# Forty expert-key blocks in plain fp32 behind chosen one-hot groups, query weights read once for most tiles, paired compares

## The chip, the cores and the metric

The kernel runs on one core of a Trainium2 chip. The metric is device microseconds of one execution; every time below is in microseconds unless it says ns. PE is TensorE, DVE is VectorE, ACT is ScalarE, POOL is GpSimd, SP issues most of the plain DMAs.

## The reference, cut to what matters

The layer takes 512 latent tokens of width 1024, runs a state-space branch and a neighbourhood-attention branch, merges them, and then runs PEER, an expert retrieval with product keys. The change touches PEER alone:

```python
def peer_ffn(h, w_q, subkeys, u_tab, v_tab):
    q = (h @ w_q).reshape(b, l, PEER_HEADS, 2, PEER_HALF)          # 8 heads, 2 halves of 128
    s = jnp.einsum('blhnd,nkd->blhnk', q, subkeys)                 # 128 keys per half
    s_top, i_top = lax.top_k(s, PEER_TOPK)                         # 16 best of each half
    cand = s_top[..., 0, :, None] + s_top[..., 1, None, :]         # 256 sums
    cand_idx = i_top[..., 0, :, None] * PEER_KEYS + i_top[..., 1, None, :]
    best, pos = lax.top_k(cand, PEER_TOPK)
    expert = jnp.take_along_axis(cand_idx, pos, axis=-1)           # 16 of 16384 experts
    gate = jax.nn.softmax(best, axis=-1)
    a = einsum('td,thkd->thk', h_blk, u_tab[expert])               # per token, 128 experts
    w = gate * gelu(a)
    return einsum('thk,thkd->td', w, v_tab[expert])
```

## The kernel before, in words

The 512 tokens are four tiles of 128. Tiles 0 to 2 (`ND = 3`, `DT = 384` tokens) are computed densely: the kernel multiplies all 16384 rows of `u_tab` with the 384 tokens, 128 rows at a time, and masks. Tile 3 is done with gathers of single rows.

*Splitting.* A weight tile is loaded on SP's queue as plain fp32 into `wraw` (3 buffers) and split by `w_split` (L171) into two fp32r parts: ACT casts `hi` (L174), DVE subtracts to get `lo` (L175). `mm3` (L449) then does three fp32r matmuls per slice of 128 inputs (hi x hi, hi x lo, lo x hi), 24 for 8 slices. `w_ahead` and `w_next` (L180, L193) walk one fixed list `wseq`: they keep the loads two to three tiles ahead and the split one tile ahead.

*Order of the stage.* `h_part` (L937) transposes the normed tiles and writes `hth` and `htl`, the split of h. `scores(h, pair)` (L1003) projects a head's two query halves for a pair of tiles: it takes two weights of the list, so all 16 query weights are loaded and split twice, once per pair. It then multiplies with the sub-keys and DVE takes the 16 best with max, find-index and match-replace. `choose(t)` (L1034) does the second top-16 of a tile and turns positions into expert numbers; its compare (L1067) of 128 positions with 16 numbers writes 2048 bf16 elements, and a multiply (L1069) of the same size follows. The program runs `scores` of tiles 0 and 1, `choose(0)`, `choose(1)`, `scores` of tiles 2 and 3, then the one-hot groups.

*One-hot groups.* `g_group(q)` (L1117) makes the gate matrix of 8 tokens: four DVE operations on 128x1024 fp16 (L1129 to L1132) write three one-hot tiles `og` (two buffers each), 16 matmuls (L1141, L1142) make a 128x128 gate matrix per token, ACT writes them out (L1144) and a DMA on ACT's queue stores them in `Gt_d` (L1147). There are 3 x 16 = 48 groups. `choose(2)` and `choose(3)` are put behind groups 14 and 33.

*Blocks that run ahead.* `u_stage(j)` (L950) is one block: 128 rows of `u_tab` against the 384 tokens, gelu, into one slot of a ring of 41. Forty blocks (`LAG`) run ahead of the main loop: 8, 12 and 18 spread over the groups of tiles 0, 1 and 2 (`NU`) and not bound to any, and two bound behind the last group. The binding is `tc.issue_after(ins)`: the block's matmuls keep behind `ins` on its engine's queue. What isn't bound, the scheduler orders by its own simulated times.

*Main loop* (L1307). For j = 0 to 124 it reads a row block of `v_tab`, splits it, multiplies the ring slot with the gates (`gch`, read back from `Gt_d`), does 18 matmuls of 512 columns into six `acc` banks, runs `u_stage` of block j + 40, and issues some gathers on POOL for tile 3. The gathers' buffers lie where the one-hot tiles were.

The line that the blocks turn on:

```python
mm3(a[:, 0:DT], w, [t[:, 0:DT] for t in hth], [t[:, 0:DT] for t in htl], KD)
```

Of the kernel before, what the change touches and what calls it, by code (L numbers as in the profile page):

```python
# [48 lines left out]
LAG = 40  # L49

GLEAD = 32
G_IN_Q = lambda q: 0
UA = 0
WQE = lambda p, i: 0
# [22 lines left out]
UKEEP = 2  # L77
NTAIL = 3
CQ = (14,33)
CB = (1,1)  # L80
BT = 3
NU = (8,12,18)
# [4 lines left out]
def tile_hybrid(ctx, tc, A, out, dbg=None):  # L87
# [92 lines left out]
    def w_ahead(load_to, split_to, eng):  # L180
# [768 lines left out]

    def u_stage(j):  # L950
# [3 lines left out]
        mm3(a[:, 0:DT], w, [t[:, 0:DT] for t in hth], [t[:, 0:DT] for t in htl], KD)  # L954
# [48 lines left out]
    def scores(h, pair):  # L1003
        qs = []
        for n in range(2):
            w = w_next(("wq", 2 * h + n), gp if WQE(pair, 2 * h + n) else dve)
            a = bank()
            mm3(a[:, 0:256], w, [t[:, pair * 256:pair * 256 + 256] for t in hth],
                [t[:, pair * 256:pair * 256 + 256] for t in htl], KD)
            q_ = tk1.tile([128, 256], F32, tag="q_", name="q_", bufs=4)  # L1010
            act.copy(q_, a[:, 0:256])
            qs.append(q_)
        sp = bank("mc" if pair * 8 + h < SPN else "tp")
        for n, q_ in enumerate(qs):
            for t in range(2):
                pe.matmul(sp[:, n * 256 + t * 128:n * 256 + t * 128 + 128], q_[:, t * 128:(t + 1) * 128], subk[:, n],
                          start=True, stop=True)
        sca = tk1.tile([128, 2, 2, 128], F32, tag="sc", name="sc", bufs=2)
        act.copy(sca.rearrange("p n a b -> p (n a b)"), sp)
        for n in range(2):  # L1020
            sc = sca[:, n]
            if h == 0 and n == 0 and pair == 0:
                DBG("sc0", sc.rearrange("p a b -> p (a b)"))
            for z in range(2):
                t = pair * 2 + z
                s_, i_ = st[:, t, n, h], it[:, t, n, h]
                dve.max(s_[:, 0:8], sc[:, z])
                dve.max_index(i_[:, 0:8], s_[:, 0:8], sc[:, z])
                s2_ = tk1.tile([128, 128], F32, tag="s2_", name="s2_", bufs=2)
                dve.match_replace(s2_, s_[:, 0:8], sc[:, z], -3.0e38)  # L1030
                dve.max(s_[:, 8:16], s2_)
                dve.max_index(i_[:, 8:16], s_[:, 8:16], s2_)

    def choose(t):  # L1034
# [15 lines left out]
        pf, u_, ab = ti("pf"), ti("u_"), ti("ab", BF16, 2, NH, 16)  # L1050
# [6 lines left out]
        dve.tensor_scalar(ab[:, 0], u_, MAGIC, MAGIC, op0=ALU.add, op1=ALU.subtract)  # L1057
        dve.scalar_tensor_tensor(ab[:, 1], ab[:, 0], -16.0, pf, op0=ALU.mult, op1=ALU.add)
# [26 lines left out]
    for h in range(NH):  # L1085
        scores(h, 0)
# [101 lines left out]

    pend_u = 0

    def pend(n, bind=False):
        nonlocal pend_u
        for _ in range(n):
            if pend_u < LAG - UKEEP:
# [209 lines left out]
```

## Time and profile before

| what | value |
|---|---|
| median of 3 runs | 1843.59 us (1843.41 to 1844.24) |
| the profiled execution's own time | 1847.01 us |
| its span, first to last instruction | 1845.2 us |
| PE busy | 1724.4 us, 93% |
| PE weight loads busy | 1507.5 us, 82% |
| DVE busy | 1468.6 us, 80% |
| ACT busy | 782.4 us, 42% |
| POOL busy | 372.9 us, 20% |
| mean granted TensorE clock | 0.968 |
| bytes moved by DMA | 426.16 MB, mean 231 GB/s |

Shares of the whole span mix stages that have different limits. The view by stretches gives each engine's busy time in a part of the span, and the share of full speed that the chip granted to TensorE's clock there. In the groups by line a row is: line, engine, operation, written tile and read tiles, shapes, count, then busy time and mean duration, then the idle time of that engine just before those instructions and what ended it. In a timeline a row is start, duration, engine and line; rows that follow each other on an engine can be merged ("x4"). The ends of matmuls are modelled, so the distance between starts is the better price.

### The profile page before, as it was taken

The numbers are of one execution on the slowest core, as the hardware profiler recorded it, in microseconds if no ns is written. First come the engines' busy times: TensorE is split into PE (matmuls) and PEld (weight loads), VectorE is DVE, ScalarE is ACT, GpSimd is POOL, SyncE is SP. The second block draws the span as 40 slices with busy tenths as digits, with TensorE's granted clock in tenths as the row PEclk, the third lists the DMA queues.
The fourth block names the chain that finished last, engine by engine and source line by source line (L and its number), as shares of the span: only waits on it lengthen the run. The fifth ranks groups of instructions, "written<-read, shape, count | busy, mean of one in ns | idle before, by whom it ended". The sixth has DMA issues, their size and how long they took to land.

```text
span 1845.2 us, 27478 instructions
## 1 busy us (share of the span) xinstructions
PE 1724.4 (93%) x9941; PEld 1507.5 (82%) x9941; DVE 1468.6 (80%) x3041; ACT 782.4 (42%) x1220; POOL 372.9 (20%) x304
## 2 busy tenths in 40 slices
PE   5999899899999899995589999999999999999997
PEld 2878677777799799994579899999999999988885
DVE  8889765875689998999888788888878788794455
ACT  6452555432464346665423333333333333333333
POOL 0001000000000000000332344544445444440012
PEclk9999999999999999995699999999999999999998
DMA  8341362885634336765799799999999999994332
GB/s 332 95 134 59 97 170 49 282 285 164 210 130 149 115 121 187 209 196 166 228 392 348 266 344 354 323 340 342 331 337 350 341 328 344 327 337 138 127 114 80
DMA packets 186328, 426.16 MB, mean 231 GB/s; under 512 B 25552, under 2 KB 91216, under 8 KB 186192
## 3 DMA queue, kind: packets, MB, share of 16 engines
q1 hardware_dynamic: 84816, 231.44, 37.1%
q0 software_dynamic: 36864, 134.23, 20.2%
q10 hardware_dynamic: 64512, 58.73, 10.2%
q8 instruction: 78, 1.28, 0.3%
q14 instruction: 58, 0.48, 0.1%
HBM read 388.72 MB, written 35.62 MB: 230 GB/s over the span
## 4 chain that ended last, share of the span: by engine, by line
PE 64%; DVE 18%; DMA 9%; issue 5%; POOL 2%; ACT 2%; SPq 0%; ACTq 0%; DVEq 0%; POOLq 0%
PE acc L1276 8%; PE acc L1275 8%; PE acc L1277 8%; PE kk L447 4%; PE yy L445 4%; PE yy L447 4%; PE yy L446 4%; PE kk L446 4%; PE kk L445 4%; DVE wlo L175 3%; DMA wm<-in_wmodT_dram 3%; PE mm L445 2%; PE mm L447 2%; DMA gu<-in_pu_dram,idx 2%; PE mm L446 2%
## 5 line engine op out<-in xcount | busy, mean ns | idle before, releaser
L174 ACT CAST whi<-wraw 128x1024 fp32r<-128x1024 f32 (+1 forms) x212 | 213.8, 1009 | 222.6 <-PE mm L446 100.4
L1158 POOL DMA_INDIRECT gu<-in_pu_dram,idx x128 | 168.9, 1319 | 598.0 <-PE mm L1142 385.3
L175 DVE TENSOR_TENSOR wlo<-wraw,whi 128x1024 fp32r<-128x1024 f32 (+1 forms) x212 | 247.6, 1169 | 36.1 <-ACT whi L174 35.5
L1158 POOL DMA_INDIRECT gu<-in_pv_dram,idx x128 | 176.8, 1382 | 192.1 <-DVE gacc L1176 165.8
L1176 DVE SCALAR_TENSOR_TENSOR gacc<-gu,av,gacc 128x1024 f32<-128x1024 f32 x127 | 162.7, 1281 | 28.1 <-DMA gu<-in_pv_dram,idx 27.7
L1257 DVE TENSOR_TENSOR wlo<-wraw,whi 128x1024 fp32r<-128x1024 f32 x128 | 157.6, 1232 | 33.5 <-ACT whi L1256 33.0
L1165 DVE SCALAR_TENSOR_TENSOR gj<-gu,hrow 128x1024 bf16<-128x1024 f32 x128 | 156.2, 1220 | 33.9 <-DMA gu<-in_pu_dram,idx 33.8
L447 PE MATMUL kk<-hth,wlo 128*128 128x384 f32 x512 | 174.2, 340 | 3.4 <-DVE wlo L175 3.4
L445 PE MATMUL kk<-hth,whi 128*128 128x384 f32 x512 | 173.4, 339 | 2.4 <-ACT ring L956 2.4
L445 PE MATMUL yy<-hth,whi 128*128 128x384 f32 x512 | 173.0, 338 | 1.5 <-ACT whi L174 1.3
L446 PE MATMUL kk<-htl,whi 128*128 128x384 f32 x512 | 173.1, 338 | 0.0
L447 PE MATMUL yy<-hth,wlo 128*128 128x384 f32 x512 | 173.0, 338 | 0.0
L446 PE MATMUL yy<-htl,whi 128*128 128x384 f32 x512 | 172.4, 337 | 0.0
L1256 ACT CAST whi<-wraw 128x1024 fp32r<-128x1024 f32 x128 | 133.7, 1046 | 59.5 <-PE kk L446 26.7
L1144 ACT ACTIVATE gs<-mm 128x512 f32<-128x512 f32 x96 | 94.1, 1090 | 56.1 <-PE mm L1142 53.1
L447 PE MATMUL mm<-hxh,wlo 128*128 128x512 f32 x256 | 103.3, 404 | 11.4 <-DVE wlo L175 11.4
L445 PE MATMUL mm<-hxh,whi 128*128 128x512 f32 x256 | 101.6, 402 | 5.6 <-ACT whi L174 3.0
L446 PE MATMUL mm<-hxl,whi 128*128 128x512 f32 x256 | 102.5, 400 | 0.0
L447 PEld LDWEIGHTS kk<-hth,wlo 128*128 128x128 f32 x512 | 96.9, 189 | 5.4 <-DVE wlo L175 4.4
L445 PEld LDWEIGHTS kk<-hth,whi 128*128 128x128 f32 x512 | 97.0, 189 | 4.5 <-ACT ring L956 2.7
L445 PEld LDWEIGHTS yy<-hth,whi 128*128 128x128 f32 x512 | 96.4, 188 | 4.6 <-ACT whi L174 1.7
L446 PEld LDWEIGHTS kk<-htl,whi 128*128 128x128 f32 x512 | 97.0, 190 | 1.7
(1912 smaller groups left out, 4258.4 us busy)
## 6 DMA issues: line engine op xcount, KB each, us to landing
wraw<-in_puT_dram SPq DMA_DIRECT2D x128, 512.0 KB
wraw<-in_pv_dram SPq DMA_DIRECT2D x128, 512.0 KB
Gt_d<-gs ACTq DMA_DIRECT2D x24, 1024.0 KB
gch<-Gt_d ACTq DMA_DIRECT2D x32, 768.0 KB
wraw<-in_win_dram SPq DMA_DIRECT2D x32, 512.0 KB
wm<-in_wmodT_dram SPq DMA_DIRECT2D x32, 512.0 KB
wraw<-in_wq_dram SPq DMA_DIRECT2D x32, 512.0 KB
wm<-in_wm_dram SPq DMA_DIRECT2D x16, 512.0 KB
```

The source lines that it names most:

```text
L174: act.copy(hi[:, :kn], raw[:, :kn])
L175: i = eng.tensor_sub(lo[:, :kn], raw[:, :kn], hi[:, :kn].bitcast(F32))
L445: pe.matmul(o, hi[:, k], xh, start=(k == 0), stop=False)
L446: pe.matmul(o, hi[:, k], xl, start=False, stop=False)
L447: pe.matmul(o, lo[:, k], xh, start=False, stop=(k == kn - 1))
L1158: gp.indirect_dma_start(out=u, out_offset=None, in_=A[tab], in_offset=bass.IndirectOffsetOnAxis(ap=ix[:, s:s + 1], axis=0))
L1165: dve.scalar_tensor_tensor(jk, u, 1.0, hrow, op0=ALU.mult, op1=ALU.mult, accum_out=av[:, s:s + 1])
L1176: dve.scalar_tensor_tensor(gacc, u, av[:, s:s + 1], gacc, op0=ALU.mult, op1=ALU.add)
L1257: dve.tensor_sub(lo, w, hi.bitcast(F32))
L1275: pe.matmul(acc[t][half], wh_[:, ts], hi[:, cs], start=(j == 0), stop=False)
L1276: pe.matmul(acc[t][half], wh_[:, ts], lo[:, cs], start=False, stop=False)
L1277: return pe.matmul(acc[t][half], wl_[:, ts], hi[:, cs], start=False, stop=(j == 127))
```

## The change

- `u_stage`: for the first 40 blocks (`NF = 40`) the raw fp32 tile is used as it is, without a split, and one plain fp32 matmul per slice takes the place of the three. The plain h of the 384 tokens is kept in `h32`, in three buffers `hq` that were free by then; two of the eight slices lie in two pieces (256 and 128 columns). `h_part` writes it (for tile 2 by an extra ACT operation per slice).
- `scores(i, tiles)` does one weight for a list of tiles: the first 4 weights (`QSP`) for the pairs as before, the other 12 for all four tiles at once (matmuls of 512 columns).
- `choose`: `ab` holds each value twice, and the compare reads pairs, as the one-hot operations do.
- Order: all scores first, with three blocks behind weights 7, 10 and 13; then `choose(0)` and 4 blocks; then the groups. `choose(1)`, `(2)`, `(3)` are bound behind groups 8, 24 and 40, each with 4 blocks bound behind that group's last matmul; of the other groups every third has one block bound behind it. 4 blocks (`UKEEP`) are kept for after the last group.
- `gacc` is allocated at its first use, in the buffer of one of the `hq` tiles.

```diff
-    wseq += [("wq", i, KD) for i in range(2 * NH)]
-    wseq += [("puT", j, KD) for j in range(UA)]
-    wseq += [("wq", i, KD) for i in range(2 * NH)]
-    wseq += [("puT", j, KD) for j in range(UA, 128)]
+    wseq += [("wq", i, KD) for i in range(QSP)] * 2
+    for i in range(QSP, 2 * NH):
+        wseq.append(("wq", i, KD))
+        if i in US:
+            wseq.append(("puT", US.index(i), KD))
+    wseq += [("puT", j, KD) for j in range(len(US), 128)]
...
-            wsp[i] = w_split(wraw.pop(i), wseq[i][2], eng)
+            raw = wraw.pop(i)
+            wsp[i] = raw if wseq[i][0] == "puT" and wseq[i][1] < NF else w_split(raw, wseq[i][2], eng)
...
+    hq = [hxp.tile([128, D], F32, tag=f"hc{i + 1}", name=f"hq{i}") for i in range(3)]
+    h32 = [(hq[k // 2][:, k % 2 * DT:k % 2 * DT + DT],) for k in range(6)]
+    h32 += [(hq[2 * i][:, 768:], hq[1][:, 768 + 128 * i:896 + 128 * i]) for i in range(2)]
...
-            f = h23[:, k] if lo else x1p.tile([128, 256], F32, tag="hf2", name="hf2", bufs=2)
+            f = h23[:, k] if lo else h32[k][0][:, 0:256]
             act.activation(f, p[:, :n], AF.Identity, bias=mod[:, 24 + k:25 + k], scale=A2[:, k:k + 1])
+            if lo:
+                act.activation(h32[k][0][:, 256:384] if k < 6 else h32[k][1], p[:, :128], AF.Identity,
+                               bias=mod[:, 24 + k:25 + k], scale=A2[:, k:k + 1])
...
-        mm3(a[:, 0:DT], w, [t[:, 0:DT] for t in hth], [t[:, 0:DT] for t in htl], KD)
+        if j < NF:
+            for k in (0, 1, 2, 3, 4, 6, 7, 5):
+                c = 0
+                for f in h32[k]:
+                    n = f.shape[-1]
+                    pe.matmul(a[:, c:c + n], w[:, k], f, start=(k == 0), stop=(k == 5))
+                    c += n
+        else:
+            mm3(a[:, 0:DT], w, [t[:, 0:DT] for t in hth], [t[:, 0:DT] for t in htl], KD)
...
+    def scores(i, tiles):
+        h, n = divmod(i, 2)
+        c = slice(tiles[0] * 128, tiles[-1] * 128 + 128)
+        nt = len(tiles)
+        w = w_next(("wq", i), gp if WQE(i) else dve)
+        a = bank()
+        mm3(a[:, 0:nt * 128], w, [t[:, c] for t in hth], [t[:, c] for t in htl], KD)
...
-            dve.tensor_tensor(ov, ab[:, n].rearrange("p h (k o) -> p (h k) o", o=1).to_broadcast([128, 128, 16]),
-                              io16.rearrange("p (o e) -> p o e", o=1).to_broadcast([128, 128, 16]), op=ALU.is_equal)
+            dve.tensor_tensor(ov.rearrange("p x (e w) -> p x e w", w=2),
+                              ab[:, n].rearrange("p x (o w) -> p x o w", o=1).to_broadcast([128, 128, 8, 2]),
+                              io16.rearrange("p (o e w) -> p o e w", o=1, w=2).to_broadcast([128, 128, 8, 2]),
+                              op=ALU.is_equal)
...
-    for h in range(NH):
-        scores(h, 0)
+    for pair in ((0, 1), (2, 3)):
+        for i in range(QSP):
+            scores(i, pair)
...
-            if chq and q == CQ[chq[0] - 2]:
-                with tc.issue_after(omark[0]) if CB[chq[0] - 2] else ExitStack():
+            if chq and q == CQ[chq[0] - 1]:
+                with tc.issue_after(omark[0]):
                     choose(chq.pop(0))
-            pend((k + 1) * nu // n - k * nu // n, t >= BT)
-
-    choose(0)
-    choose(1)
-    pend(UA)
-    for h in range(NH):
-        scores(h, 1)
+                pend(CU, gmark[0])
+            elif q % GU == 0:
+                pend(1, gmark[0])
+
+    for i in range(QSP, 2 * NH):
+        scores(i, (0, 1, 2, 3))
+        pend(i in US)
     close_pool(t1cm)
     gpl_open()
+    choose(0)
+    pend(CU)
```

## Rows read from the trace of the kernel before

**Rows 1.** Stretches: busy us (instructions) by engine; granted clock, DMA share, GB/s.

```profile
500.00:630.00 130.00, 121.41 (x935) 116.87 (x935) 124.80 (x569) 65.39 (x108) 0.38 (x2) 0.98 0.42 135
630.00:820.00 190.00, 185.81 (x1329) 176.79 (x1329) 179.40 (x456) 113.20 (x146) 0.00 (x0) 1.00 0.57 168
820.00:910.00 90.00, 47.97 (x410) 41.00 (x409) 83.00 (x188) 48.58 (x55) 7.14 (x6) 0.61 0.61 181
910.00:941.00 31.00, 23.41 (x107) 21.83 (x106) 22.00 (x47) 9.03 (x12) 13.89 (x9) 0.83 1.02 386
941.00:1660.00 719.00, 716.37 (x3612) 650.62 (x3612) 600.78 (x859) 250.46 (x353) 324.70 (x241) 1.00 0.93 336
```

**Rows 2.** Groups by line, DVE, 500:910 (busy us, mean ns | idle before).

```profile
L175 DVE TENSOR_TENSOR wlo<-wraw,whi 128x1024 fp32r<-128x1024 f32 x70 | 84.9, 1214 | 2.9 <-ACT whi L174 2.8
L1129 DVE TENSOR_TENSOR og<-ioe,slots 128x1024 f16<-128x1024 f16 x48 | 32.9, 686 | 8.7 <-PE mm L1142 8.6
```

**Rows 3.** Timeline (start, us): last group on DVE, first `acc` matmul.

```profile
907.22 0.69 DVE L1132 TENSOR_TENSOR og<-og,slots 128x1024 f16<-128x1024 f16 x1
...
936.32 0.77 PE L1275 MATMUL acc<-whi,wh__9933 128*128 128x512 f32 x1 [5.76 <-issue]
```

**Rows 4.** Timeline of DVE: splits, old compare, one-hot operation, multiply.

```profile
598.85 2.33 DVE L175 TENSOR_TENSOR wlo<-wraw,whi 128x1024 fp32r<-128x1024 f32 x2
...
877.14 2.29 DVE L1067 TENSOR_TENSOR oh<-ab,io 128x2048 bf16<-128x2048 bf16 x1
879.35 0.69 DVE L1129 TENSOR_TENSOR og<-ioe,slots 128x1024 f16<-128x1024 f16 x1
879.95 0.69 DVE L1130 TENSOR_TENSOR og<-ioe,slots 128x1024 f16<-128x1024 f16 x1
...
883.96 1.22 DVE L1069 TENSOR_TENSOR oh<-oh,itf 128x2048 bf16<-128x2048 bf16 x1
885.09 0.69 DVE L1131 TENSOR_TENSOR og<-og,slots 128x1024 f16<-128x1024 f16 x1
```

**Rows 5.** Timeline of PE, matmuls of a block as split before.

```profile
742.14 0.34 PE L447 MATMUL yy<-hth,wlo 128*128 128x384 f32 x1
...
743.36 0.34 PE L445 MATMUL yy<-hth,whi 128*128 128x384 f32 x1
```

**Rows 6.** PE timeline: plain fp32, 256 and 128 columns (last: min/median/max ns).

```profile
232.71 0.60 PE L710 MATMUL mm<-kTC,q 128*128 128x256 f32 x2
...
233.14 0.59 PE L711 MATMUL mm<-kTC,q 128*128 128x256 f32 x2
...
545.87 0.61 PE L1016 MATMUL tp<-subk,q__5653 128*128 128x128 f32 x4
...
L1016 PE MATMUL mc<-subk,q__5426 x4: 271/274/275, 527.1 to 527.4; 128*128 128x128 f32 x4
```

**Rows 7.** Timeline of PE, one-hot matmuls at the high and the low clock level.

```profile
746.86 0.22 PE L1142 MATMUL mm<-og,og 128*128 128x128 f16 x1
...
747.08 0.22 PE L1142 MATMUL mm<-og,og 128*128 128x128 f16 x1
...
896.27 0.31 PE L1141 MATMUL mm<-og,og 128*128 128x128 f16 x1
...
896.81 0.31 PE L1142 MATMUL mm<-og,og 128*128 128x128 f16 x1
```

**Rows 8.** Timeline of PE, split matmuls of 512 and of 256 columns.

```profile
444.98 0.39 PE L445 MATMUL mm<-hxh,whi 128*128 128x512 f32 x1
...
446.12 0.39 PE L447 MATMUL mm<-hxh,wlo 128*128 128x512 f32 x1
...
544.79 0.28 PE L447 MATMUL mm<-hth,wlo 128*128 128x256 f32 x1
...
545.75 0.28 PE L446 MATMUL mm<-htl,whi 128*128 128x256 f32 x1
```

**Rows 9.** Matmuls on the tile hth, query part (first and last start).

```profile
L445 PE MATMUL mm<-hth,whi x256: 274/283/420, 511.4 to 634.3; 128*128 128x256 f32 x128
```

More of the change, by code (lines that the diff above doesn't have):

```diff
@@ L49 @@
 LAG = 40
+NF = 40
+QSP = 4
 GLEAD = 32
 G_IN_Q = lambda q: 0
-UA = 0
-WQE = lambda p, i: 0
+US = (7, 10, 13)
+WQE = lambda i: 0
 CHE = lambda t, n: 0
@@ L76 @@
 UENG = lambda j: 0
-UKEEP = 2
+UKEEP = 4
 NTAIL = 3
[L79 to L82, printed above, removed]
+CQ = (8,24,40)
+CU = 4
+GU = 3
 G_IN_J = lambda j: 0 if j<4 else 2+(j%2==0)
@@ L1001, in ti @@
         return tk2.tile([128, *(extra or (NH, 16))], dt, tag=name, name=name, bufs=1)
[L1003 to L1032, printed above, removed]
@@ new lines, in scores @@
+    def scores(i, tiles):
[5 more added lines that the diff above has]
+        mm3(a[:, 0:nt * 128], w, [t[:, c] for t in hth], [t[:, c] for t in htl], KD)
+        q_ = tk1.tile([128, 512], F32, tag="q_", name="q_", bufs=3)
+        act.copy(q_[:, 0:nt * 128], a[:, 0:nt * 128])
+        sp = bank("tp")
+        for z in range(nt):
+            zs = slice(z * 128, z * 128 + 128)
+            pe.matmul(sp[:, zs], q_[:, zs], subk[:, n], start=True, stop=True)
+        sc = tk1.tile([128, 4, 128], F32, tag="sc", name="sc", bufs=3)
+        act.copy(sc[:, 0:nt].rearrange("p a b -> p (a b)"), sp[:, 0:nt * 128])
+        for z, t in enumerate(tiles):
+            s_, i_ = st[:, t, n, h], it[:, t, n, h]
+            dve.max(s_[:, 0:8], sc[:, z])
+            dve.max_index(i_[:, 0:8], s_[:, 0:8], sc[:, z])
+            s2_ = tk1.tile([128, 128], F32, tag="s2_", name="s2_", bufs=2)
+            dve.match_replace(s2_, s_[:, 0:8], sc[:, z], -3.0e38)
+            dve.max(s_[:, 8:16], s2_)
+            dve.max_index(i_[:, 8:16], s_[:, 8:16], s2_)
@@ L1049, in choose @@
             dve.max_index(pos[:, h, 8:16], best[:, h, 8:16], c2)
-        pf, u_, ab = ti("pf"), ti("u_"), ti("ab", BF16, 2, NH, 16)
+        pf, u_, ab = ti("pf"), ti("u_"), ti("ab", BF16, 2, 128, 2)
         act.copy(pf, pos)
@@ L1056, in choose @@
         dve.tensor_scalar(u_, pf, 0.0625, -0.46875, op0=ALU.mult, op1=ALU.add)
-        dve.tensor_scalar(ab[:, 0], u_, MAGIC, MAGIC, op0=ALU.add, op1=ALU.subtract)
-        dve.scalar_tensor_tensor(ab[:, 1], ab[:, 0], -16.0, pf, op0=ALU.mult, op1=ALU.add)
+        u2, pf2 = (z.rearrange("p h (k o) -> p (h k) o", o=1).to_broadcast([128, 128, 2]) for z in (u_, pf))
+        dve.tensor_scalar(ab[:, 0], u2, MAGIC, MAGIC, op0=ALU.add, op1=ALU.subtract)
+        dve.scalar_tensor_tensor(ab[:, 1], ab[:, 0], -16.0, pf2, op0=ALU.mult, op1=ALU.add)
         if t < ND:
@@ L1150, in tile_hybrid @@
     ix = idx
-    gacc = hxp.tile([128, D], F32, tag="hc1", name="gacc")
+    gacc = None
     gup = [None]
@@ L1171, in g_v @@
     def g_v(s):
+        nonlocal gacc
         u = gath("pv", s)
         if s == 0:
+            gacc = hxp.tile([128, D], F32, tag="hc1", name="gacc")
             dve.tensor_scalar(gacc, u, av[:, 0:1], None, op0=ALU.mult)
@@ L1189, in tile_hybrid, with pend @@
     pend_u = 0
-    def pend(n, bind=False):
+    def pend(n, after=None):
         nonlocal pend_u
@@ L1194, in pend, with g_tile @@
             if pend_u < LAG - UKEEP:
-                with tc.issue_after(gmark[0]) if bind else ExitStack():
+                with tc.issue_after(after) if after is not None else ExitStack():
                     u_stage(pend_u)
                 pend_u += 1
-    chq = [2, 3]
-    def g_tile(t, nu):
+    chq = [1, 2, 3]
+    def g_tile(t):
         n = 128 // TB
@@ L1205, in g_tile @@
             g_group(q)
[L1206 to L1207 removed]
+            if chq and q == CQ[chq[0] - 1]:
+                with tc.issue_after(omark[0]):
                     choose(chq.pop(0))
[L1209 to L1215 removed]
+                pend(CU, gmark[0])
[4 more added lines that the diff above has]
+        pend(i in US)
     close_pool(t1cm)
     gpl_open()
+    choose(0)
+    pend(CU)
     for t in range(ND):
[L1219 removed]
+        g_tile(t)
     while chq:
```

1 line of the change is left out of this document (removed).

## The prediction

> **What bounds the kernel now.** I read the stretches first [rows 1]. The long loop from 941 to 1660 us keeps PE busy 716 of 719 us at a granted clock of 1.00, so it is PE's, and the change does not touch what it does per block. What the change touches is the stage before it, from 500 to 910. There DVE is busy 124.8 + 179.4 + 83.0 = 387.2 of 410 us, while PE, in the last 90 us, is busy 48 us at a granted clock of 0.61. So DVE sets the end of that stage and PE only fills it. The groups by line say what DVE does there [rows 2]: 70 weight splits (L175), 48 each of the four one-hot operations, and the choosing. The only wait that counts is 8.7 us before the first one-hot operation, on PE (the one-hot buffers were still being read). The loop cannot begin before the last group is through: its last DVE operation starts at 907.2, the first `acc` matmul at 936.3 [rows 3]. If the last group comes earlier, everything behind it moves by the same amount.
>
> **What a DVE operation is worth.** Durations on DVE overlap by some 0.08 us, so I price by start-to-start [rows 4]: a split 1.12 us (two end 2.33 after the first starts, one lasts 1.21 by [rows 2]), the old compare 879.35 - 877.14 = 2.21, the multiply on 128x2048 bf16 885.09 - 883.96 = 1.13, one one-hot operation (128x1024) 0.60.
>
> **Removed from DVE.**
> - The splits of the blocks that run ahead. Of 70 splits in the stage, 32 are the query weights' (16 weights, twice); 38 are blocks. 38 x 1.12 = 42.6 us. The matching casts on ACT (38 more) lie off the path: ACT is busy 48.6 of 90 us even in the last stretch [rows 1].
> - 12 of the 32 query splits: 12 x 1.12 = 13.4 us. With them go 12 loads of 512 KB on SP's queue, at a DMA share of 0.42 [rows 1], hidden; nothing queued behind them waits.
> - The 8 compares. No row shows the paired form in bf16, but the one-hot operations use the same pairing in 16 bit and the multiply of the same 2048 elements takes 1.13. Bounds: 1.13 below, 2.21 above. I take 1.13, the nearest row: 8 x 1.08 = 8.6 us.
> - Added: the two operations that write `ab` now write 256 elements instead of 128, 8 in all. Between nothing and one 0.60 operation each (4.8 us); they are short, I take 1.
>
> Sum 42.6 + 13.4 + 8.6 - 1 = 63.6 us less DVE work.
>
> **PE, the cover.** A block now has 24 matmuls of 384 columns, 7 starts apart in 1.22 us, 0.174 each [rows 5]: 24 x 0.174 = 4.18 us. The new block has 6 full-fp32 matmuls of 384 columns and 2 each of 256 and 128. No row has 384, but 256 columns are there: two of L710 start at 232.71 and after, the next, of L711, at 233.14, so 0.43 / 2 = 0.215 per matmul; and four with 128 columns, of 0.275 each, are through in 0.61, so (0.61 - 0.275) / 3 = 0.112 [rows 6]. By the columns 384 is 0.322: 6 x 0.322 + 2 x (0.215 + 0.112) = 2.59 us. Bounds from the rows: not under one pass of the split kind (8 x 0.174 = 1.4), and above, twice 2.59 = 5.17 if the rate does not carry over. I take 2.59: it is the same data type and the nearest shape. **A rule against this**: the Trainium skill, FP8 and Floating Point Precision, section TensorE Precision Notes, says true FP32 takes four passes through the array; that would make the block about 5.1 us (estimate from that page), slower on PE than the split. By [rows 6] the trace does not agree: 256 columns take 0.215 us in plain fp32 against 0.120 for one pass of the split kind [rows 8], two passes and not four.
>
> The blocks: three stand in the query stage (behind weights 7, 10, 13), 4 behind `choose(0)`, 4 each at groups 8, 24 and 40, and one at every third group otherwise (15), which is 34; 2 follow unbound, 4 after the last group. So 31 lie beside the groups. PE there has 48 x 16 = 768 small matmuls at 0.055 (four starts in 0.22 us, at the 2.4 GHz level, [rows 7]) = 42 us, and 31 x 2.59 = 80 us: 122 us. The stage's second part lasts some 220 us for DVE (from 625 to about 845, below), so PE covers all of it: the PE time of the blocks costs nothing. If DVE were gone as cover, those 80 us would be on the path.
>
> **The query part** changes owner. Matmuls of 512 columns start 0.228 apart (five in 1.14), of 256 columns 0.120 (eight in 0.96) [rows 8], so a wide weight costs PE 24 x 0.228 + 4 x 0.112 = 5.92 us and a narrow one 24 x 0.120 + 2 x 0.112 = 3.10. After: 8 x 3.10 + 12 x 5.92 + 3 x 2.59 = 104 us; from 511.4 [rows 9], with an allowance of 10 us for the transposes of tiles 2 and 3, the queries end about 625. Before they ended at 634.3 on PE [rows 9] with two `choose` done meanwhile by DVE. Now `choose(0)` cannot start until the queries end, so DVE may idle a little beside PE, and has nothing else to do while `choose(0)` makes its trips through ACT. This new idle is between 0 and the whole old idle once more (410 - 387.2 = 22.8 us); I take 10. Against it the 8.7 us of waits on the one-hot buffers go [rows 2], since PE is no longer full. What is late next, where that wait goes, is DVE itself.
>
> **Waits that are added.** Each block's matmuls stand behind one group's matmuls, on PE's queue alone. Queued behind the block is the next group, and DVE waits for that only when it is two groups ahead (two one-hot buffers); two groups are 8 x 0.60 = 4.8 us, the block 2.59, so no wait. `choose(1..3)` were bound before, too (two of them), now three. On SP's queue a block's raw tile is held by PE until the block is done, where the split freed it before; only later weights are behind it. On POOL nothing moves: the gathers still wait for the last group. `gacc` takes over a buffer that block 39 reads, long free by then. The eight extra ACT evictions (128x128) sit in the first 40 us, where ACT is busy half the time [rows 1].
>
> **The opening of the loop**, 29 us from last group to first `acc` [rows 3], runs at a DMA share of 1.02 and 386 GB/s [rows 1]. Four blocks are kept for it instead of two, so up to two more tiles of 512 KB load there: 2 x 1.36 = 2.7 us, bounds 0 and twice that. I take 3.
>
> **Sum**: 63.6 + 8.7 - 10 - 3 = 59 us gained. The profiled execution took 1847.0 us (span 1845.2), 3.4 above the median of the runs; I subtract from both: 1788 for such an execution, 1784 for the median. A measurement of this kernel can tell 0.2% (3.7 us).
>
> **Rivals.**
> 1. *PE's clock stays low in the second part.* For: with groups alone PE fell to a granted clock of 0.61 [rows 1], small matmuls 0.108 apart (five starts in 0.54), the 1.2 GHz level [rows 7]. Against: PE was then idle nearly half the time, and now has 122 us instead of 42 to do in 220. Price: all at the low level, 768 x 0.108 + 31 x 5.17 = 83 + 160 = 243 us, 23 over DVE's 220, and the six last blocks (31 us) outlast the opening by some 4: 1811. Half of it gives about 1797.
> 2. *Plain fp32 needs twice the time of my row's rate* (5.17 per block at the high level). For: no row has 384 columns. Against: the rows with 128 and with 256 columns [rows 6]. Beside the groups 42 + 160 = 202 stays under 220; the query part grows by 3 x 2.59 = 8, the six last blocks fill 31 us of an opening of 29, with some 4 us lost: 1796. This is what the Trainium skill's page named above would give.
> 3. *Slower: blocks and one-hots take turns.* If the order comes out so that the next group's one-hot operations wait for each block to finish, every one of the 31 adds its length to DVE's line: 31 x 2.59 = 80 us against the 59 gained, 1865. It decides from 59 / 31 = 1.9 us of wait per block. For: the one wait that exists is exactly this one (8.7 us on PE's reads, [rows 2]). Against: with blocks of 4.18 us between the groups it came to 8.7 us for 48 groups.
> 4. *The paired compare is not faster*: 8.6 us less gained, 1792.
>
> **How the numbers follow.** Forecast 0.66 (own range 1768 to 1798), rival 1 0.17, rival 2 0.06, rival 4 0.05, rival 3 0.06. The range goes from 1765 (all of the new idle and the opening's loss absent, 13 us, and some of the old idle gone too) to 1815 (rival 1 in full, with 4 us over). Left out are rival 3 and the ends of the others, under 2 in 10. Faster: all but rival 3 and a rest for causes I don't see, 0.93; same 0.01; slower 0.06.
>
> **What would show it.** 160 splits at L175 in place of 212; compares of about 1.2 us; block matmuls of 384 columns lasting about 0.49 (0.17 us of pipeline as in [rows 6] plus 0.32); queries' end near 625, last group near 845, first `acc` near 875, a loop as long as before; DVE still busy over 90% between 500 and 845, waits on one-hot buffers small. Wrong if the last group comes after 870, if DVE's idle is due to PE, or if the time from last group to first `acc` grows by more than 10 us.

## The result, and the profile after

The changed kernel takes 1909.64 us in the median of four executions (1904.12 to 1913.81), the kernel before 1843.5 (1843.36 to 1844.24): a ratio of 1.0357, 95% interval 1.0341 to 1.0373. Slower by 3.6%, where 1784 us was forecast.

The profiled execution of the changed kernel took 1904.1 us (span 1902.4, 57.2 more than before). Its stretches have the columns of [rows 1]. They are cut where the queries have ended (640), behind `choose(0)` and the first groups (680), in the late groups (910), at the first `acc` matmul (984), and after 719 us of loop:

```profile
500.00:640.00 140.00, 137.13 (x751) 115.84 (x750) 107.99 (x557) 53.31 (x93) 0.38 (x2) 0.99 0.28 91
640.00:680.00 40.00, 23.23 (x100) 15.61 (x99) 32.39 (x135) 8.16 (x14) 0.00 (x0) 0.79 0.15 44
680.00:910.00 230.00, 192.37 (x1164) 134.42 (x1162) 163.21 (x434) 100.73 (x127) 4.04 (x5) 0.91 0.52 152
910.00:984.00 74.00, 50.85 (x238) 33.80 (x237) 46.34 (x87) 16.54 (x24) 28.11 (x24) 0.85 0.98 345
984.00:1703.00 719.00, 713.86 (x3593) 647.95 (x3594) 586.32 (x835) 247.01 (x348) 302.81 (x228) 1.00 0.91 329
...
500.00:941.00 441.00, 372.72 (x2103) 278.95 (x2102) 328.01 (x1166) 168.79 (x240) 17.18 (x17) 0.91 0.44 135
```

The same view of the kernel before, up to its last one-hot operation:

```profile
500.00:908.00 408.00, 353.20 (x2655) 332.66 (x2655) 385.97 (x1209) 226.07 (x306) 6.80 (x8) 0.91 0.53 159
```

The loop is what it was in [rows 1]. The loss lies ahead of it, and the two lines from 500 on show its kind. From 500 to its last one-hot operation (940.9) DVE is busy 328.0 of 441 us; before it was 386.0 of 408. So 58 us of work have gone (63.6 were forecast), and DVE's idle time has grown from 22 to 113 us: 91 - 58 = 33 us later. Two of DVE's groups by line, from 620 to 990:

```profile
L1143 DVE TENSOR_TENSOR og<-ioe,slots 128x1024 f16<-128x1024 f16 x48 | 33.1, 690 | 64.4 <-PE mm L1156 62.7 <-ACT slots L1125 1.5
L1078 DVE TENSOR_TENSOR oh<-ab,io 128x2048 bf16<-128x2048 bf16 x8 | 9.4, 1218 | 0.0
```

The last of the four one-hot lines, and the first `acc` line for the loop's first two blocks, each in the view of its line; the last line is the second block of the kernel before:

```profile
L1146 DVE TENSOR_TENSOR og<-og,slots x48: 669/683/693, 671.6 to 940.9; 128x1024 f16<-128x1024 f16 x48
...
L1293 PE MATMUL acc<-whi,wh__8831 x6: 628/628/763, 983.9 to 986.1; 128*128 128x512 f32 x6
...
L1293 PE MATMUL acc<-whi,wh__8894 x6: 388/395/502, 1001.0 to 1002.3; 128*128 128x512 f32 x6
...
L1275 PE MATMUL acc<-whi,wh__9996 x6: 388/394/397, 942.9 to 946.3; 128*128 128x512 f32 x6
```

The wait for PE's reads of the one-hot tiles was 8.6 us [rows 2] and is 62.7. The last group comes at 940.9 for 907.2, the second block of the loop at 1001.0 for 942.9: 33.7 us are lost up to the last group and 24.4 behind it, together 58.1, where the span grew by 57.2.

One run-ahead block by itself, in the view of its line (least, median and longest ns, first and last start):

```profile
L968 PEld LDWEIGHTS kk<-hq,wraw x20: 188/190/193, 565.5 to 570.2; 128*128 128x128 f32 x20
L968 PE MATMUL kk<-hq,wraw x20: 272/484/488, 565.7 to 570.6; 128*128 128x384 f32 x12, 128*128 128x256 f32 x4, 128*128 128x128 f32 x4
```

The program has ten matmuls here; the engine ran twenty, each with its weight load. A plain fp32 matmul is two instructions, so the block costs 12 x 0.322 + 4 x (0.215 + 0.112) = 5.17 us, twice my price, and not less than the split block's 4.18 but more. In the run e5 below, blocks back to back start at 648.73, 653.91 and 659.09: 5.18 apart.

How groups and blocks lie on PE, in its timeline:

```profile
739.62 0.28 PE L1155 MATMUL mm<-og,og 128*128 128x128 f16 x2 [1.99 <-DVE og L1145]
...
742.36 0.31 PE L1156 MATMUL mm<-og,og 128*128 128x128 f16 x1
742.46 7.66 PE L968 MATMUL yy<-hq,wraw 128*128 128x384 f32 x20
749.96 0.22 PE L1156 MATMUL mm<-og,og 128*128 128x128 f16 x1
...
752.03 0.22 PE L1156 MATMUL mm<-og,og 128*128 128x128 f16 x1
754.24 0.39 PE L1155 MATMUL mm<-og,og 128*128 128x128 f16 x2 [1.99 <-ACT gs L1158]
...
756.88 7.28 PE L968 MATMUL kk<-hq,wraw 128*128 128x384 f32 x20
```

and on DVE:

```profile
742.71 0.69 DVE L1143 TENSOR_TENSOR og<-ioe,slots 128x1024 f16<-128x1024 f16 x1 [0.94 <-PE mm L1156]
...
744.76 0.69 DVE L1146 TENSOR_TENSOR og<-og,slots 128x1024 f16<-128x1024 f16 x1
750.99 0.69 DVE L1143 TENSOR_TENSOR og<-ioe,slots 128x1024 f16<-128x1024 f16 x1 [5.54 <-PE mm L1156]
...
753.50 1.29 DVE L1145 TENSOR_TENSOR og<-og,slots 128x1024 f16<-128x1024 f16 x2
754.70 1.28 DVE L1146 TENSOR_TENSOR og<-og,slots 128x1024 f16<-128x1024 f16 x2
```

The two take turns. While a block holds PE, DVE finishes the one group that it has a free buffer for, at 745.4, and stands until PE has read again at 751.0. After the block PE works off the two groups that are ready in 2 us, then itself waits until DVE has written the third (752.0 to 754.2). PE's row names ACT's copy of the gates (`gs`) there; DVE's first L1145 operation, which the third group needs, ends within 0.05 us of PE's start (753.50 + 0.69), and the same pause at 739.62 names DVE. The run e8 below tells the two apart: with a third one-hot buffer the pauses that name ACT are still there, but last 0.3 us in most rows and not 2. Only behind that third group comes the next block. A round of three groups takes 742.46 to 756.88 = 14.4 us (the like rounds up to 878 take 11.8 to 14.7), for which DVE has 3 x 2.4 = 7.2 us of work. These two blocks are also slow: 7.3 and 7.7 us where the twenty matmuls take 5.4 (5.18 from start to start) at full clock. PE had just been idle, its matmuls ahead of the block start 0.107 us apart (the 1.2 GHz level) and those behind it 0.055 (2.4 GHz), and the granted clock of the stretch is 0.91.

### The profile page after: what moved, and what is told of

Same layout as the page of the kernel before. It is cut to its first block, busy times and chain, and to the rows that moved or that the text cites. A ratio compares the mean times of both kernels' runs of the same rounds, so it can differ in the third digit from the quotient of the medians.

```text
span 1902.4 us, 26392 instructions
## 1 busy us (share of the span) xinstructions
PE 1764.9 (93%) x9493; PEld 1465.5 (77%) x9493; DVE 1407.7 (74%) x2989; ACT 732.5 (39%) x1168; POOL 362.2 (19%) x304
## 4 chain that ended last, share of the span: by engine, by line
PE 77%; DVE 13%; DMA 5%; ACT 2%; issue 2%; POOL 0%; SPq 0%; POOLq 0%; DVEq 0%; ACTq 0%
PE acc L1293 9%; PE acc L1294 9%; PE acc L1295 9%; PE kk L968 4%; PE yy L968 4%; PE mm L451 4%; PE mm L449 4%; PE mm L450 3%; PE kk L451 3%; PE kk L449 3%; PE kk L450 3%; PE yy L449 3%; PE yy L450 3%; PE yy L451 3%; DMA wm<-in_wmodT_dram 2%
## 5 line engine op out<-in xcount | busy, mean ns | idle before, releaser
L178 DVE TENSOR_TENSOR wlo<-wraw,whi 128x1024 fp32r<-128x1024 f32 (+1 forms) x160 | 184.5, 1154 | 57.2 <-ACT whi L177 51.5
L177 ACT CAST whi<-wraw 128x1024 fp32r<-128x1024 f32 (+1 forms) x160 | 159.0, 995 | 156.6 <-PE mm L450 96.8
L1179 DVE SCALAR_TENSOR_TENSOR gj<-gu,hrow 128x1024 bf16<-128x1024 f32 x128 | 156.1, 1220 | 33.7 <-DMA gu<-in_pu_dram,idx 33.2
L451 PE MATMUL kk<-hth,wlo 128*128 128x384 f32 x352 | 118.9, 338 | 1.2 <-DVE wlo L178 1.2
L968 PE MATMUL yy<-hq,wraw 128*128 128x384 f32 (+2 forms) x400 | 118.2, 454 | 1.9 <-ACT ring L973 1.9
L451 PE MATMUL yy<-hth,wlo 128*128 128x384 f32 x352 | 118.2, 336 | 0.0
L449 PE MATMUL yy<-hth,whi 128*128 128x384 f32 x352 | 118.1, 335 | 0.0
L450 PE MATMUL yy<-htl,whi 128*128 128x384 f32 x352 | 118.0, 335 | 0.0
L968 PE MATMUL kk<-hq,wraw 128*128 128x384 f32 (+2 forms) x400 | 116.0, 447 | 0.0
L968 PEld LDWEIGHTS yy<-hq,wraw 128*128 128x128 f32 x400 | 74.5, 205 | 38.3 <-issue 9.7
L1155 PE MATMUL mm<-og,og 128*128 128x128 f16 x384 | 57.4, 233 | 46.8 <-ACT gs L1158 23.7
```

What stands on the lines that cost most here:

```text
L177: act.copy(hi[:, :kn], raw[:, :kn])
L178: i = eng.tensor_sub(lo[:, :kn], raw[:, :kn], hi[:, :kn].bitcast(F32))
L449: pe.matmul(o, hi[:, k], xh, start=(k == 0), stop=False)
L450: pe.matmul(o, hi[:, k], xl, start=False, stop=False)
L451: pe.matmul(o, lo[:, k], xh, start=False, stop=(k == kn - 1))
L968: pe.matmul(a[:, c:c + n], w[:, k], f, start=(k == 0), stop=(k == 5))
```

## The experiments

Eighteen kernels, each against runs of the kernel before on the same chip. DVE's wait is that for PE's reads of the one-hot tiles; "last" is the start of DVE's last one-hot operation and "opening" the time from there to the first `acc` matmul of the loop's second block, both from each run's profile.

| kernel | ratio to before, 95% | wait | last | opening |
|---|---|---|---|---|
| before | 1 | 8.6 | 907.2 | 35.7 |
| the change | 1.0357 (1.0341 to 1.0373) | 62.7 | 940.9 | 60.1 |
| e1 before, plain fp32 | 1.0044 (1.0022 to 1.0066) | 59.9 | 918.4 | 37.1 |
| e4 before, paired compares | 0.998 (0.9964 to 0.9996) | 5.5 | 899.5 | 38.4 |
| e13 before, blocks bound | 1.0081 (1.0063 to 1.01) | 13.2 | 917.0 | 39.9 |
| e2 change, split | 1.0208 (1.0183 to 1.0233) | 43.4 | 934.2 | 44.8 |
| e3 change, half a block | 0.9942 (0.9919 to 0.9964) | 24.3 | 877.3 | 47.6 |
| e5 change, unbound | 1.0012 (0.9998 to 1.0025) | 44.7 | 895.1 | 52.2 |
| e7 change, last six split | 1.0232 (1.0211 to 1.0254) | 59.1 | 942.5 | 41.4 |
| e8 change, three buffers | 1.0047 (1.0033 to 1.0062) | 17.8 | 887.8 | 60.2 |
| e9 change, old queries | 1.0282 (1.0252 to 1.0312) | 62.0 | 940.1 | 56.0 |
| e17 change, every second group | 1.0072 (1.0055 to 1.0089) | 39.0 | 901.4 | 53.3 |
| e18 change, no block in queries | 1.0226 (1.0209 to 1.0243) | 59.7 | 927.0 | 57.6 |
| e10 change, unbound and split | 0.9988 (0.9971 to 1.0005) | 8.3 | 893.4 | 42.7 |
| e14 as e10, old queries | 0.997 (0.9953 to 0.9987) | 10.0 | 896.6 | 40.5 |
| e11 as e8, last six split | 0.9999 (0.9983 to 1.0014) | 18.5 | 891.8 | 49.8 |
| e12 as e11, blocks earlier | 0.9898 (0.988 to 0.9916) | 36.1 | 878.0 | 37.2 |
| e15 as e12, all split | 0.9979 (0.9966 to 0.9992) | 21.1 | 886.1 | 39.6 |
| e16 as e12, two buffers | 0.9927 (0.9897 to 0.9957) | 40.7 | 890.4 | 41.4 |
| e19 as e12, every second block split | 0.9859 (0.9834 to 0.9884) | 17.4 | 870.4 | 40.2 |

**Price or order.** The first four take the change apart: plain fp32 in the old order; the new order with split blocks; the new order with blocks at the price that I had forecast; the compares.

```diff
 # e1: before, with the raw tile and h32 for blocks 0 to 39
+    raw if wseq[i][0] == "puT" and wseq[i][1] < NF else w_split(raw, ...)
 # e2: the change
-NF = 40
+NF = 0
 # e3: the change; half of each block's sum is left out
-            for k in (0, 1, 2, 3, 4, 6, 7, 5):
+            for k in (0, 1, 2, 5):
 # e4: before, with the paired ab, compare and nothing else
```

> The kernel before with one part of the change alone: all 40 blocks in plain fp32 (raw tile, h32), in the old order, unbound, NU 8/12/18; query weights twice, old compares. Theory A (a plain fp32 matmul is two instructions, a block 5.18 us of PE and no split on DVE; the loss of the full change comes from where the blocks stand, not from their kind): DVE loses 38 x 1.12 = 43 us, PE gains 40 us of which 42 us were idle between 820 and 910, so both end close together, the last group comes 25 to 40 us earlier and the time is 1805 to 1825. Theory B (plain fp32 blocks are the whole loss: 40 x 1.0 us more on PE, and raw tiles held by PE keep loads back at the loop's opening): 1850 to 1900.

> The changed kernel with NF = 0: order, bindings, wide queries and paired compares as changed, but the blocks split in three fp32r passes as before (4.18 us of PE, a split on DVE). Theory A (order and bindings make DVE and PE take turns): still slower than before, 1865 to 1900, with over 40 us of waits of the first one-hot operation on PE. Theory B (plain fp32 is the whole loss): 1815 to 1835, since 13 us of query splits and 9 us of compares are gone.

> The changed kernel in which the 40 blocks that run ahead use only four of the eight slices of h (each of 384 columns, 8 matmul instructions), so a block takes 8 x 0.32 = 2.6 us of PE, the price that the prediction used; the other four slices are left out of these blocks. If the size of the block was the only error of the prediction: 1775 to 1800, waits of the first one-hot operation under 15 us. If DVE and PE take turns whatever the block's size: 1909.6 - 37 x 2.6 = about 1815 to 1830, with waits of some 30 us.

> The kernel before with the paired compares alone. DVE sets the stage's end: 8 x 1.08 us less on DVE, about 1835 to 1838. If PE sets it: 1843, no change.

Both matter, and together they cost more (3.6%) than one by one. Plain fp32 by itself gains nothing (e1: 0.4% slower), though it takes 40 splits from DVE. My theory A (1805 to 1825 us) missed: the last group came 11 us later, not 25 to 40 earlier, since PE was full from 640 to 860, 219.8 of 220 us in e1's view by stretches:

```profile
640.00:680.00 40.00, 40.00 (x165) 27.40 (x164) 39.09 (x174) 8.67 (x15) 0.00 (x0) 1.00 0.29 92
680.00:740.00 60.00, 59.88 (x380) 42.89 (x379) 35.38 (x65) 28.63 (x38) 0.00 (x0) 1.00 0.57 167
740.00:800.00 60.00, 59.91 (x347) 42.23 (x346) 46.82 (x132) 26.36 (x36) 0.00 (x0) 1.00 0.62 176
800.00:860.00 60.00, 60.00 (x381) 42.93 (x380) 33.97 (x66) 27.50 (x34) 0.00 (x0) 1.00 0.65 185
```

The new order by itself costs 2.1% (e2, as its theory A said). At my price the change would have been a gain (e3), but of 0.6%, not of the 3.2% forecast: DVE still waits 24.3 us for PE's reads. So in this order the size of the block is 4.15 points of the miss, and the remaining 2.65 were wrong whatever the size. The paired compares alone gain 0.2% (e4), less than half of their 8.6 us.

**What in the order.** Four changes of one thing each: no binding, three buffers, the old query part, the last six blocks split.

```diff
 # e5
-                pend(CU, gmark[0])
+                pend(CU)
-                pend(1, gmark[0])
+                pend(1)
 # e8
-tag=f"og{i}", name=f"og{i}", bufs=2
+tag=f"og{i}", name=f"og{i}", bufs=3
-tag="slots", name="slots", bufs=2
+tag="slots", name="slots", bufs=1
 # e9: wseq lists all 16 weights twice; scores(i, (0, 1)), choose(0), scores(i, (2, 3))
 # e7
-NF = 40
+NF = 34
```

> The changed kernel with its run-ahead blocks in the same places of the program, but not bound behind a given group. Theory O, the binding fixes the order that is bad: unbound, blocks slip into PE's idle time earlier (in the 22 us that PE idles around choose(0), 640 to 680 us, above all), the wait for PE's reads falls below 45 us and the time is 1860 to 1885 us. Rival T, the order hardly moves because the block follows its group anyway: within 10 us of the changed kernel, 1895 to 1915 us.

> The changed kernel with three buffers for each one-hot tile instead of two (one instead of two for the slot columns, to make room). Theory T, the two buffers make blocks and one-hots take turns: DVE gets 2.4 us more of its work done while a block of 5.2 to 7.5 us holds PE, so of the 62.7 us that DVE waited for PE's reads at least 30 go, PE idles less between groups and its clock rises, and the time is 1850 to 1880 us (two new waits at the slot columns, 2 to 4 us each, are in it). Rival P, PE's own time is the limit from 680 to 910 us whatever DVE does (it was busy 192 of 230 us there): at most 15 us go, 1892 to 1910 us.

> The changed kernel with the query part of before alone put back: each query weight loaded and split twice, first for tiles 0 and 1, then for 2 and 3, with choose(0) between the passes (the other three choices stay where the change puts them). Theory Q, the wide weights cost more than the 13.4 us of splits that they save, since choose(0) then stands alone at the end of the queries (DVE busy 140 of 180 us from 500 to 680): the last one-hot group comes 10 to 25 us earlier and the time is 1880 to 1897 us. Rival, DVE's idle time there is only moved and PE sets the pace afterwards: no gain or a loss of up to 15 us by the splits, 1905 to 1922 us.

> The changed kernel with its last six run-ahead blocks (34 to 39: two behind the last groups and four after them) as split blocks again, the other 34 in plain fp32. Theory L, these six blocks make the opening of the loop longer (43 us from the last group to the first acc matmul against 29 before, and the second j later still): PE holds each raw tile until its block is done, and the loop's loads stand behind them; with splits the tiles come free early, the opening falls to 30 to 36 us and the time by 8 to 20 us, 1886 to 1901 us. Rival G, the opening is set by the gathers and by the evictions behind the late groups: six splits more on DVE and the same opening, 1903 to 1915 us.

The third buffer takes 45 us of the wait and 3.1 points of time, with the blocks where they were: the turns are real, and with the blocks in these places they hang on the buffers. Unbound the loss goes as well, in another way, and further (1845 us) than theory O said. The view by stretches of e5:

```profile
500.00:640.00 140.00, 137.12 (x749) 116.23 (x748) 110.07 (x547) 55.80 (x98) 0.38 (x2) 0.99 0.29 96
640.00:680.00 40.00, 40.00 (x164) 27.55 (x163) 32.61 (x150) 8.78 (x16) 0.00 (x0) 1.00 0.30 93
680.00:826.00 146.00, 145.92 (x911) 104.02 (x910) 101.47 (x278) 69.89 (x89) 0.00 (x0) 1.00 0.61 177
826.00:910.00 84.00, 57.99 (x413) 45.23 (x411) 73.85 (x179) 45.44 (x54) 2.99 (x3) 0.70 0.61 175
```

The blocks now fill PE without a gap from 640 to 826, at full clock; DVE idles 52 of those 186 us instead, and sets the end from 826 on. First PE is the bound and DVE idles, then DVE is the bound and PE idles (58.0 of 84 us busy).

e7 changes nothing up to the last group (942.5) and takes 19 us from the opening: the six blocks in plain fp32 do lengthen it, as theory L said. The timeline of SP's queue (start, us, line, written and read, count) in the change:

```profile
942.75 12.53 SPq L188 DMA_DIRECT2D wraw<-in_puT_dram  x3
965.71 0.91 SPq L1263 DMA_DIRECT2D wraw<-in_pv_dram  x2
966.71 6.30 SPq L188 DMA_DIRECT2D wraw<-in_puT_dram  x3
```

and in e7:

```profile
941.43 16.11 SPq L188 DMA_DIRECT2D wraw<-in_puT_dram  x4
961.37 1.62 SPq L1263 DMA_DIRECT2D wraw<-in_pv_dram  x3
966.19 8.11 SPq L188 DMA_DIRECT2D wraw<-in_puT_dram  x2
```

From 941 to the first load of `in_pv_dram` SP issues four tiles in 20 us in e7, three in 23 us in the change. Counted over the whole queue, the change has by then issued the tiles of 40 blocks (0 to 39), e7 those of 43. Of the waits of SP's queue from 940 to 1003, PE's reads of raw tiles (L968) are 25.5 + 5.3 us in the change and 5.5 us in e7. The tile of block 40 is issued at 966.71 only, and PE stands still before its matmuls, just ahead of the first `acc` matmul:

```profile
982.86 0.69 PE L449 MATMUL kk<-hth,whi 128*128 128x384 f32 x1 [10.21 <-ACT whi L177]
```

That PE holds the raw tiles is thus seen in the trace. It isn't the only wait: in the change the first load of `in_pv_dram` also waited 10.2 us for the last store of the gates (`Gt_d`). No run changed the raw buffers alone, so the share of each stays open.

e9 is 0.75 points better than the change, but not as expected: the groups begin and end when they did (last one at 940.1). What its profile shows of the gain, 4 us, lies in the opening (56.0), and I can't say why.

**Binding alone, and the rest alone.** e13 binds the blocks of the kernel before; e10 is the change unbound and split; e11 puts two remedies together; e12 also moves blocks to where PE idled.

```diff
 # e13: before
-BT = 3
+BT = 0
 # e10: e5 with NF = 0;  e11: e8 with NF = 34;  e12: e11 and
-US = (7, 10, 13)
+US = ()
     choose(0)
-    pend(CU)
+    pend(7)
-GU = 3
+GU = 2
```

> The kernel before with one thing changed: its 38 run-ahead blocks beside the groups are each bound behind the group they follow in the program (split blocks, everything else as it was). Theory B, the binding alone makes turns: a group then waits for the whole block of 4.2 us ahead of it, the wait for PE's reads (8.7 us before) rises to 25 us or more, PE idles between and its granted clock falls, and the time is 1855 to 1885 us. Rival, the binding hurts only with the longer plain fp32 block: below 1848 us, with 8 to 15 us of that wait.

> The changed kernel with all 40 blocks split again and none bound: what is left is the wide query weights, the paired compares, and the places of the blocks and choices. Theory B: with the binding gone PE fills its idle time around choose(0) with blocks and the rest hides under DVE; of DVE's work 22 us less than before is left, so 1820 to 1840 us. Rival Q, the queries with choose(0) alone behind them take back what the wide weights save: 1840 to 1860 us. The difference to the unbound kernel in plain fp32 (1845 us) is what plain fp32 is worth in this order: theory, it gains nothing or little, since PE was full from 640 to 826 us there.

> The changed kernel with three buffers for each one-hot tile (one for the slot columns) and its last six blocks split: two edits that gave 58 us (three buffers) and 20 us (six splits) alone. If they act at different places (the groups; the opening of the loop) they add: 1825 to 1840 us. If the six blocks cost what they did only because everything before them was late, or six splits land on a DVE that is now full: 1845 to 1855 us.

> As the kernel with three buffers and six split blocks, and the blocks earlier where PE idles: none in the query part (PE was full there and idled 17 us during choose(0)), seven unbound behind choose(0) instead of four, and one at every second group instead of every third, so that only four are left after the last group. Theory: the queries end 15 us earlier, choose(0) with them, and the last group at 865 to 880 us; 1800 to 1828 us. Rival, PE's time is the limit from the first group on (29 blocks of 5.2 us and 48 groups are 195 us, DVE's groups and choices about 185): the gain in the queries is given back, 1830 to 1850 us.

Binding costs the kernel before 0.8%, in the range given, but theory B had the wrong place for it: the wait is 13.2 us, not 25. A bound block can't fill PE's time between the queries and the first group. In the stretches of e13 PE is busy 4.1 of these 40 us, where the same view of before, the second line, has 36.7:

```profile
640.00:680.00 40.00, 4.11 (x14) 2.76 (x14) 39.53 (x181) 4.35 (x11) 0.00 (x0) 0.50 0.05 13
...
640.00:680.00 40.00, 36.71 (x214) 36.06 (x213) 40.00 (x131) 19.25 (x27) 0.00 (x0) 1.00 0.37 111
```

The blocks come later instead. e10 is no faster than before (theory B had 1820 to 1840 us, measured 1841.61), so wide queries, paired compares and the new places together gain nothing that can be told, though DVE has 22 us less to do. e11 gains 0.5 points on e8, not 1.25: the two remedies overlap. e12 is 1.0% faster than before, as expected.

**Plain fp32, buffers, queries in an undisturbed order.**

```diff
 # e15: e12 with NF = 0;  e16: e12 with og bufs=2, slots bufs=2;  e14: e10 with the query part of e9
```

> The kernel with three buffers and earlier blocks (1824 us), with all 40 blocks split instead of six. Theory P, plain fp32 is worth something once blocks and groups no longer take turns: 34 splits of 1.12 us on DVE are 38 us more, PE has 34 us less (5.18 against 4.18 per block), and since PE set the pace there (58 of 60 us in each stretch from 680 to 860) part of the loss comes back: 1832 to 1855 us. Rival, the two kinds of block are worth the same, as in the unbound order (1845 and 1842 us): 1818 to 1830 us. Below 1818 us the split blocks are the better ones.

> The kernel with three buffers and earlier blocks (1824 us), with two buffers for each one-hot tile and two for the slot columns, as in the changed kernel. Theory T, two buffers make bound blocks and groups take turns wherever the blocks stand: 29 bound blocks, 2.4 us of DVE's work lost for each at most, so 1860 to 1895 us. Rival, the earlier places of the blocks did it and the third buffer adds little: 1824 to 1845 us.

> The unbound kernel with all 40 blocks split (1842 us), with the query part of before: each query weight split twice, choose(0) between the two passes. What is left of the change is the paired compare and the places of the blocks and of three choices. Theory Q, the wide query weights gain nothing here, since the 13.4 us of splits that they save come back as DVE's idle time before the first group: 1832 to 1845 us. Rival, they are worth the 13.4 us of splits or more: 1850 to 1860 us.

My theory that two buffers make turns wherever the blocks stand fell: with two of them, e16 is only 0.3 points behind e12 (the intervals overlap), where 2 to 4 were expected. The turns need two buffers *and* the places that the change gave the blocks. And plain fp32 is worth 0.8 points once blocks and groups no longer hinder each other (e12 against e15, 34 blocks), and otherwise costs 0.2 (unbound, e5 against e10), 0.4 (in the old order, e1) or 1.5 points (bound as in the change, against e2). The wide query weights are worth nothing (e14 against e10, intervals overlap).

**Which of the places.**

```diff
 # e17: the change
-GU = 3
+GU = 2
 # e18: the change
-US = (7, 10, 13)
+US = ()
     choose(0)
-    pend(CU)
+    pend(7)
 # e19: e12, and for blocks 0 to 33
-        if j < NF:
+        if j < NF and j % 2 == 0:
```

> The changed kernel with one number changed: a bound block at every second group instead of every third (all 40 in plain fp32, two buffers, the query part as changed). Theory C, the cadence makes the turns: with two buffers DVE has two groups written when a block ends, so at every second group PE goes from block to two groups to block without a pause (7.5 us for two groups), while at every third it stands still until DVE has written the third (14.3 us for three groups, clock down to 0.7 to 0.9); the 48 groups take 20 to 40 us less, fewer blocks are left for the opening, and the time is 1845 to 1880 us. Rival, what helped was to keep blocks out of the query part or the six splits: 1890 to 1912 us.

> The changed kernel with no block in the query part and seven instead of four unbound behind choose(0), at every third group as changed. Theory C, this moves the groups' start earlier by at most the 15.5 us of the three blocks, less what PE idled during choose(0) anyway: 1892 to 1905 us, and the waits between the groups stay at 55 us or more. Rival, PE's clock is what matters (PE is then full up to the first group): waits below 45 us and 1850 to 1885 us.

> The kernel with three buffers and earlier blocks (1824 us; all 40 split: 1839 us), with every second block plain fp32 and the others split. With plain blocks alone PE sets the pace of two groups (7.1 to 7.5 us), with split ones DVE does (two groups and a split, 5.9 us) and idles elsewhere; mixed, the third buffer lets DVE use its time in the plain ones: 1810 to 1823 us. Rival, no time can be carried from one block to the next: between the two, 1826 to 1836 us.

One number, every second group instead of every third, takes 2.85 points off the change. PE's timeline of e17:

```profile
753.98 5.40 PE L968 MATMUL kk<-hq,wraw 128*128 128x384 f32 x20
759.22 0.33 PE L1155 MATMUL mm<-og,og 128*128 128x128 f16 x3
...
761.08 0.22 PE L1155 MATMUL mm<-og,og 128*128 128x128 f16 x1 [0.36 <-ACT gs L1158]
...
761.52 0.86 PE L968 MATMUL yy<-hq,wraw 128*128 128x384 f32 x2
```

The round of two groups takes 761.52 - 753.98 = 7.54 us. When a block ends, two groups are ready (two buffers), and behind the second stands the next block: in this round PE doesn't wait for DVE, its one pause is 0.36 us. At every third group it must wait for one that DVE could not start. That is theory C, its time came in its range (1857.66 us), and the stretch of the groups in e17 says the same:

```profile
680.00:860.00 180.00, 173.40 (x1151) 125.14 (x1150) 137.88 (x351) 92.51 (x118) 0.00 (x0) 1.00 0.63 185
```

The same stretch in e19:

```profile
680.00:860.00 180.00, 166.75 (x1247) 140.28 (x1245) 161.12 (x418) 108.45 (x135) 0.00 (x0) 1.00 0.66 196
```

In e17 PE is busy 173 of 180 us at a granted clock of 1.00: PE is now the bound, and DVE's wait of 39.0 us only shows that. A part of e17's gain is that fewer blocks are left for the opening (53.3 for 60.1). e18 gains 1.3 points, more than theory C gave it, with the waits unchanged at 59.7: the last group comes 14 us earlier, and the opening shortens a little. In e19 half the blocks are split again, which shifts work from PE to DVE until both are busy some 90%: 1816.57 us against 1843.38, a ratio of 0.9859. That is the fastest kernel here and beats before and change; its lead over e12 is hardly clear of the noise (0.9834 to 0.9884 against 0.988 to 0.9916).

## Why the prediction was wrong

- *The work removed from DVE*, 63.6 us by start-to-start prices: right. By the groups by line the splits up to the last group fell by 63.1 us of busy time and the compares by 8.9; DVE's whole busy time fell by only 58, since 12 us more of tile 3's products (`gj`) came ahead of the last group. 160 splits are left, as said, the loop is as long as it was, and the paired compare lasts 1.218 us for 2.285.
- *The price of a block*, 2.59 us: this step failed, the block takes 5.18. 0.322 per instruction of 384 columns was right, but I counted statements of the program where the rows count instructions. [rows 6] held the answer: `q__5426`, for which the program has two matmuls, shows x4. A slice of 384 columns takes 2 x 0.322 = 0.644 us, 3.7 times the 0.174 of one pass of the split kind. The Trainium skill (FP8 and Floating Point Precision, section TensorE Precision Notes) gives true FP32 four passes through the array, and the trace agrees with it. "Two passes and not four" compared one of two instructions with one pass. The same slip is in the query part: its sub-key matmuls cost twice the 0.112 us (7 us more in all) and its three blocks 8 us more, and the queries ended at 639, not 625.
- *"The block 2.59, so no wait"* failed too, and at that very price: e3 has it, and waits 24.3 us; at the true price the wait is 62.7. With two buffers a round goes without a pause if the next block stands two groups on (e17) and not if it stands three on (the change); I compared the block with two groups of DVE's work and did not lay one round of three groups out in order.
- *"PE covers all of it"*: I set PE's total (122 of 220 us) against DVE's. By the same totals rival 2 cost 12 us at twice the price. Totals hide what alternates: in the change both engines idle in the same stretch, PE 38 and DVE 67 us of the 230 from 680 to 910.
- *The new idle in the queries*, 10 us of 0 to 22.8: outside the bounds. From 500 to 680 DVE idled 5.2 us and now 39.6, 34 more, since the queries are PE's and `choose(0)` stands alone behind them. So the term for the 12 query splits was lost, as e14 shows.
- *The opening*, 3 us of 0 to 5.4: it is 13.9 us longer to the first `acc` matmul (43.0 for 29.1) and 24.4 to the second block's. I priced two loads more. That PE holds the raw tiles I had seen and put at nothing ("only later weights are behind it"); with the last six blocks split, 19 of these 24 us go (e7), and those later weights are what the loop begins with.
- *The rivals.* Rival 3, blocks and one-hots take turns, is what happened, and I gave it 0.06 on the ground that blocks of 4.18 us had cost 8.7 us of waits; but those were unbound, and what isn't bound moves to where PE is free. Its sum, one whole block length for each of 31 blocks, would be 160 us at the true price; the idle grew by 91, since DVE does get a group done in each round's block. Rival 2's premise held. Rival 1 is a part: 40 blocks were busy 232 us (5.80 each) where e16's 34 took 183.5 (5.40), so the clock cost the blocks some 16 us. A low clock alone is not the loss: e3, with half the block, was granted 0.83 from 680 to 860, the change 0.91 there, and e3 is the faster. No run held the clock up with the order as it was, so its whole share stays open. Rival 4 was wrong.

By the runs the parts don't add: no binding 3.45 points, three buffers 3.1, every second group 2.85, no blocks in the queries 1.3, the last six split 1.25, the old queries 0.75, of a loss of 3.57. Each of the first three, which undo the round of some 14 us, takes most of it.

## What to carry to other kernels

Before a row becomes the price of a statement, count how many of the row's instructions one statement made. Where one engine feeds another through n buffers and a long job is put between, write out one whole round in order of time, since the two engines' totals don't show that they alternate. With two buffers the job had to stand two hand-overs apart here, not three. An order tied down by hand takes from the scheduler the places where the job would have been free: e13 lost 0.8% by that alone.

## What was not expected of the hardware

A plain fp32 matmul ran as two pairs of weight load and matmul, 0.322 us of pace each at 384 columns, and so slower than the three fp32r matmuls it replaced (5.18 against 4.18 us per block); what it gave here is the splits that DVE and ACT were spared. Of the ten blocks from 742 to 878 that began behind a group for which PE had waited 2 us, eight lasted 6.2 to 7.7 us and two 5.4; the granted clock was 0.91 in the stretch of the groups and 0.79 around `choose(0)`. In e17, in the round above, PE's gaps are 0.36 us, its blocks last 5.4, and the granted clock from 680 to 860 was 1.00.
